# Batch normalisation, loads and stores on two rings: stores no longer wait for the store before them

## The chip, the cores and the metric

One core of a Trainium2 chip. The time is the device time of the slowest core of one execution, in microseconds (us), here that of the only core. Executions of one kernel on one chip lie within some 0.1 to 0.3% of each other; a run is compared with the runs of the kernel before on its own chip.

## The reference

`x` is float32 of 32 x 256 x 128 x 128 (537 MB); the result has the same shape.

```python
mean = running_mean.reshape(1, -1, 1, 1)
var = running_var.reshape(1, -1, 1, 1)
return gamma * (x - mean) / np.sqrt(var + eps) + beta      # gamma, beta reshaped likewise
```

For one channel this is `x * scale + shift`. The work is the traffic: each value is read once and written once.

## The kernel before

Comments on the lines are added for this text.

`x` is seen as 64 tiles of 128 partitions x 16,384 values (8.39 MB). Three buffers in the on-chip memory hold three tiles; VectorE (DVE) works in place. SP issues the loads (its ring is q1), ACT the stores (its ring is q10). Left out: the computation of scale and shift at the start, some 12 us beside the first load.

```python
NBUF = 3
...
for i in range(1, NT):                       # SP: loads
    s, turn = i % NBUF, i // NBUF
    if turn:
        nc.sync.wait_ge(stored[s], 16 * turn)            # L97: the buffer's last store has landed
    inst = nc.sync.dma_start(out=bufs[s][:], in_=xr[i]).then_inc(loaded[s], 16)     # L98
    if i >= 2:                                           # and the load before has landed
        inst._wait_ge(loaded[(i - 1) % NBUF], 16 * ((i - 1) // NBUF + 1))
...
def store(i, after):                         # ACT: stores
    s = i % NBUF
    inst = nc.scalar.dma_start(out=outr[i], in_=bufs[s][:]).then_inc(stored[s], 16) # L137
    inst._wait_ge(done, after)                           # the tile's compute is done

def turn_of_store(i):
    nc.scalar.wait_ge(stored[(i - 1) % NBUF], 16 * ((i - 1) // NBUF + 1))

compute(0, left)._wait_ge(early, 16)
compute(0, right)._wait_ge(loaded[0], 16)
store(0, 2)
for i in range(1, last):
    compute(i)._wait_ge(loaded[i % NBUF], 16 * (i // NBUF + 1))     # DVE
    turn_of_store(i)                                                # ACT: one store at a time
    store(i, i + 2)
...                                          # the last tile: 9216 columns on DVE, 7168 on ACT
store(last, last + 3)
```

## Time and profile before

| | kernel before |
|---|---|
| time, median of 3 runs | 2483.66 us (2483.18 to 2484.57) |
| span of the profiled run | 2484.7 us |
| busy: DVE, ACT | 23%, 0% |
| DMA engines busy, 30 to 2454 us | 1.00 |
| one load, issue to landing (median of 63) | 38.6 us |
| store issued after its tile's landing (median) | 16.9 us |

The last row holds the wait that the change takes out; the prediction shows the lines behind the table.

A second source is used throughout, the DMA packet records of the trace: start, length, size and ring of each packet, without the engine's number. Sums over all packets divided by 16 are "per engine". The order on one engine I rebuilt, by joining each packet to the engine whose last packet ended nearest its start; engines whose packets end at the same moment can be swapped in this, so sums are safer than any one row. In the rows below, L is a 65,536-byte packet of a load, S one of a store, l and s the small packet that ends an engine's part of a transfer; the number is the start in us, in the last two digits before the point. The kernel before, two of its 16 engines, around the landing at 1020.4 us and the store's issue at 1037.4:

```
L10.3 S12.7 L15.1 S17.6 l20.0 S20.0 S22.4 L24.8 S27.2 L29.6 S32.0 L34.5 s36.9 L36.9 L39.3 S41.7 L44.1 S46.5
L11.0 S13.4 l15.8 S15.8 S18.3 S20.7 S23.1 L25.5 S27.9 L30.3 s32.7 L32.8 L35.2 L37.6 L40.0 S42.4 L44.8 S47.2
```

Each ring has a gap between two transfers, and each gap is filled with packets of the other ring.

### The profile page before, as it was taken

To read this page: it belongs to the slowest core of one execution; us is meant where nothing else is said; L and a number is where in the kernel's file an instruction comes from. 1 tells how busy PE (TensorE), PEld (TensorE's weight loads), DVE (VectorE), ACT (ScalarE), POOL (GpSimd) and SP (SyncE) were. 2 spreads that over 40 slices of the span, in tenths; PEclk is the share of its full clock that TensorE was granted. 3 is DMA by queue.
4 is the path that set the end of the run, shared out by engine and by line. 5 is a ranking of instruction groups with operands and counts; after the bars stand their busy time and mean duration, and the time that the engine had idled before them with its cause. 6 is when DMAs were issued, how large, how long until landed. Compare 5 with 4: busy or idle time off the path is not lost.

```text
span 2484.7 us, 389 instructions
## 1 busy us (share of the span) xinstructions
DVE 564.0 (23%) x76; ACT 7.9 (0%) x3; POOL 0.2 (0%) x4
## 2 busy tenths in 40 slices
DVE  3121221212212222122221221212212122121221
ACT  0000000000000000000000000000000000000001
POOL 0000000000000000000000000000000000000000
DMA  9999999999999999999999999999999999999999
GB/s 422 423 439 434 430 436 435 437 428 437 435 436 432 433 438 429 436 434 431 434 427 437 437 426 439 436 432 430 436 438 430 433 427 438 430 430 437 436 426 406
DMA packets 18707, 1073.84 MB, mean 432 GB/s; under 512 B 2128, under 2 KB 2192, under 8 KB 2192
## 3 DMA queue, kind: packets, MB, share of 16 engines
q1 hardware_dynamic: 9488, 536.94, 50.1%
q10 hardware_dynamic: 9216, 536.88, 49.9%
q14 instruction: 3, 0.02, 0.0%
HBM read 536.94 MB, written 536.87 MB: 432 GB/s over the span
## 4 chain that ended last, share of the span: by engine, by line
DMA 99%; ACT 0%; SPq 0%; issue 0%; DVE 0%; DVEq 0%
DMA t<-in_x_dram 99%; ACT t L154 0%; SPq L87 0%; DVE rows L85 0%; SPq L91 0%; DVE eps_t L103 0%; DVEq L190 0%; SPq L66 0%
## 5 line engine op out<-in xcount | busy, mean ns | idle before, releaser
L126 DVE TENSOR_SCALAR t<-t,scale_t,shift_t 128x16384 f32<-128x16384 f32 (+2 forms) x65 | 560.5, 8624 | 1886.5 <-DMA t<-in_x_dram 1886.4
L154 ACT ACTIVATE t<-t,shift_t,scale_t 128x7168 f32<-128x7168 f32 x1 | 6.4, 6361 | 2442.7 <-DMA t<-in_x_dram 2442.7
L104 DVE STREAM_TRANSPOSE turned<-rows 32x1024 f32<-32x1024 f32 x1 | 1.2, 1233 | 7.1 <-DMA rows<-in_running_mean_dram 7.1
L111 ACT ACT_TABLE_LOAD x1 | 1.3, 1283 | 0.9 <-SPq L66 0.9
L85 DVE MEMSET rows<- 32x1024 f32 x1 | 0.9, 912 | 1.2 <-SPq L66 1.2
L109 DVE COPY par<-turned 32x8 f32<-32x8 f32 x4 | 0.6, 162 | 0.1
L111 ACT ACTIVATE std_t<-par,eps_t 128x2 f32<-128x2 f32 x1 | 0.3, 295 | 9.2 <-DVE par L109 9.2
L118 DVE RECIPROCAL rstd_t<-std_t 128x2 f32<-128x2 f32 x1 | 0.2, 166 | 0.4 <-ACT std_t L111 0.4
L121 DVE TENSOR_TENSOR shift_t<-par,ms_t 128x2 f32<-128x2 f32 x1 | 0.2, 163 | 0.0
L120 DVE TENSOR_TENSOR ms_t<-par,scale_t 128x2 f32<-128x2 f32 x1 | 0.2, 161 | 0.0
L119 DVE TENSOR_TENSOR scale_t<-par,rstd_t 128x2 f32<-128x2 f32 x1 | 0.2, 161 | 0.0
L179 POOL MEMSET const-bfloat16-1.0<- 128x1 bf16 x1 | 0.1, 102 | 0.0
L179 POOL MEMSET const-uint8-127<- 128x1 uint8 x1 | 0.1, 101 | 0.0
L179 POOL MEMSET const-float32-0.0<- 128x1 f32 x1 | 0.1, 99 | 0.2 <-issue 0.2
L179 POOL MEMSET const-float32-1.0<- 128x1 f32 x1 | 0.1, 98 | 0.0
L103 DVE MEMSET eps_t<- 128x1 f32 x1 | 0.1, 59 | 0.1
## 6 DMA issues: line engine op xcount, KB each, us to landing
t<-in_x_dram SPq DMA_DIRECT2D x1, 6144.0 KB, 19.4
t<-in_x_dram SPq DMA_DIRECT2D x1, 2048.0 KB, 7.6
out_dram<-t ACTq DMA_DIRECT2D x64, 38.6
t<-in_x_dram SPq DMA_DIRECT2D x63, 38.6
rows<-in_running_var_dram SPq DMA_DIRECT2D x1, 16.0 KB, 6.4
rows<-in_gamma_dram SPq DMA_DIRECT2D x1, 16.0 KB, 6.2
rows<-in_beta_dram SPq DMA_DIRECT2D x1, 16.0 KB, 5.9
rows<-in_running_mean_dram SPq DMA_DIRECT2D x1, 16.0 KB, 5.9
```

The lines of the kernel that those rows point to most:

```text
L85: zeroed = step(nc.vector.memset(rows[:], 0.0))
L103: step(nc.vector.memset(eps_t[:], eps))
L104: step(nc.vector.transpose(out=turned[:], in_=rows[:]), fetched, 16 * NPAR)
L109: placed = step(nc.vector.tensor_copy(out=flat[q * B : (q + 1) * B], in_=blocks[:, :, q, 0]))
L111: nc.scalar.activation(out=std_t[:], in_=var_t, func=mybir.ActivationFunctionType.Sqrt, bias=eps_t[:], scale=1.0,)._wait_ge(vec, placed).t ...
L118: step(nc.vector.reciprocal(out=rstd_t[:], in_=std_t[:]), act, 1)
L119: step(nc.vector.tensor_mul(out=scale_t[:], in0=gamma_t, in1=rstd_t[:]))
L120: step(nc.vector.tensor_mul(out=ms_t[:], in0=mean_t, in1=scale_t[:]))
L121: ready = step(nc.vector.tensor_sub(out=shift_t[:], in0=beta_t, in1=ms_t[:]))
L126: return nc.vector.tensor_scalar(out=t[:, cols], in0=t[:, cols], scalar1=scale_t[:, cb : cb + 1], scalar2=shift_t[:, cb : cb + 1], op0=myb ...
L154: nc.scalar.activation(out=t[:, VCOLS:], in_=t[:, VCOLS:], func=mybir.ActivationFunctionType.Identity, bias=shift_t[:, cb : cb + 1], scale ...
L179: nc = _bacc.Bacc("TRN2", target_bir_lowering=False, num_devices=1)
```

## The change

Its intent: a store is queued as soon as its tile is computed. ACT then never stands in front of a finished tile, and the stores' ring need not run empty between two stores. The loads keep their rule of one at a time.

```diff
-        def turn_of_store(i):
-            nc.scalar.wait_ge(stored[(i - 1) % NBUF], 16 * ((i - 1) // NBUF + 1))
-
         compute(0, left)._wait_ge(early, 16)
         compute(0, right)._wait_ge(loaded[0], 16)
         store(0, 2)
         for i in range(1, last):
             compute(i)._wait_ge(loaded[i % NBUF], 16 * (i // NBUF + 1))
-            turn_of_store(i)
             store(i, i + 2)
```

## The prediction

> **What bounds the kernel now.** I read the page's totals first, then its DMA part, then the waits of the two engines that issue transfers, then the order of time in one steady stretch and at the end. The page:
>
> ```profile
> DVE 564.0 (23%) x76; ACT 7.9 (0%) x3; POOL 0.2 (0%) x4
> ...
> DMA  9999999999999999999999999999999999999999
> ...
> q1 hardware_dynamic: 9488, 536.94, 50.1%
> q10 hardware_dynamic: 9216, 536.88, 49.9%
> q14 instruction: 3, 0.02, 0.0%
> HBM read 536.94 MB, written 536.87 MB: 432 GB/s over the span
> ```
>
> No compute engine is busy for more than 23% of the span. The 16 DMA engines are at 90% or more in all 40 slices, and the two rings (q1 the loads, issued by SP; q10 the stores, issued by ACT) share them 50.1% to 49.9%: together all of it. The stretches of time say how full this is (columns: stretch, its length, busy time of three engines, clock, DMA share, GB/s):
>
> ```profile
> 0.00:2.00 2.00, 0.79 (x1) 1.10 (x1) 0.20 (x4) 1.00 0.07 16
> 2.00:30.00 28.00, 11.79 (x13) 0.47 (x2) 0.00 (x0) 1.00 1.05 444
> 30.00:1020.00 990.00, 220.32 (x26) 0.00 (x0) 0.00 (x0) 1.00 1.00 433
> 1020.00:2010.00 990.00, 229.13 (x26) 0.00 (x0) 0.00 (x0) 1.00 1.00 433
> 2010.00:2454.40 444.40, 96.94 (x11) 0.00 (x0) 0.00 (x0) 1.00 1.00 433
> 2454.40:2461.40 7.00, 5.08 (x1) 6.36 (x1) 0.00 (x0) 1.00 0.91 393
> 2461.40:2481.40 20.00, 0.00 (x0) 0.00 (x0) 0.00 (x0) 1.00 0.97 419
> 2481.40:2484.70 3.30, 0.00 (x0) 0.00 (x0) 0.00 (x0) 1.00 0.00 0
> ```
>
> The DMA share is 1.00 from 30 us to 2454 us. What is idle lies at the two ends: 2 us before the first packet, 3.3 us after nearly the last. Every tile is 8.39 MB, moved in and out. In the DMA packet records each engine moves a tile as eight packets of 65,536 bytes; a packet takes 2.418 us, and successive packets of one engine start 2.414 us apart, for loads and stores alike. So a tile costs each engine 16 packets, 16 x 2.414 = 38.6 us, which is the step of the chain that ended last. 64 tiles x 38.6 = 2472 us is the floor that the traffic sets, and the span is 2485: at most 13 us (0.5%) can be had by any reordering of the same bytes.
>
> The waits, and one steady stretch:
>
> ```profile
> SPq L98 <- DMA t<-in_x_dram: 1378.8, 62, 48.0
> SPq L97 <- DMA out_dram<-t: 1009.0, 61, 16.8
> ```
> ```profile
> 1020.46 155.17 SPq L98 DMA_DIRECT2D t<-in_x_dram  x5
> 1020.47 8.81 DVE L126 TENSOR_SCALAR t<-t,scale_t,shift_t 128x16384 f32<-128x16384 f32 x1 [29.85 <-DMA t<-in_x_dram]
> 1037.40 155.24 ACTq L137 DMA_DIRECT2D out_dram<-t  x5
> ```
>
> A load is released at 1020.46 by the landing of the load before it (L98 has the later wait; the buffer's store, L97, had landed about 22 us earlier: 38.6 less 16.5). The compute ends at 1029.28, but its store goes only at 1037.40, when the store before it has landed: that wait of 8.1 us is what the change removes.
>
> **What the Trainium skill says.** The page "DMA: Bandwidth & Descriptors", section "Queues, rings and completion order", says that each DMA engine goes round robin between the rings it has work for, a whole packet at a time. The trace agrees: in the packet records an engine alternates load, store, load, store; where one ring is empty between two transfers (last landing, semaphore, next issue, first packet) it takes 3 to 5 packets in a row of the other ring, and in the steady stretch no engine shows an idle gap worth naming. Its section "Issuing engines are not separate DMA queues" says that transfers issued from several engines run on the same 16 DMA engines, and that this saves only issue time; the trace agrees (one store's issue is 0.34 us on ACT). Its section "Where 436 GB/s comes from" gives 435.2 GB/s as the ceiling of the ports into the on-chip memory; 16 engines at 65,536 bytes per 2.414 us are 434 GB/s, so the kernel already stands at it.
>
> **The change part by part.** It takes out 62 waits of ACT, nothing else: bytes, packets, compute and the loads' waits stay.
>
> 1. What the waits cost now. 62 x 8.1 us = 502 us of a store held back, all beside a busy DMA. A store that is held leaves its ring empty for a moment, and the engines then take load packets: nothing is lost on the path.
>
> 2. What comes in the steady state. A store is queued when its compute is done, behind the rest of the store before it in the same ring. The stores' ring has no gap at first while the loads' ring still has one (2 to 4 packets more for stores per turn), so stores gain on loads. That ends within a few tiles, when a store has nothing ahead of it on arrival: then it is compute, 8.8 us after the load's landing, that starts a store, and both rings have gaps of like size again. The period stays 16 packets, 38.6 us. Median landing time of stores goes from 38.6 to something between 38.6 and 46.7 (8.1 more at the front), back towards 38.6 once the gain is used up. The gap of the loads is still filled: at a load's end an engine has now 5 to 6 store packets left of the previous store; with stores 8.1 us earlier, about 3.4 of 16 slots, half of them stores, it has about 3 to 4 left, and the gap needs 3 to 5. It is near the edge, but the engines that need 5 are those ahead on loads, thus behind on stores.
>
> 3. What it does to the end. Before:
>
> ```profile
> 2415.80 8.81 DVE L126 TENSOR_SCALAR t<-t,scale_t,shift_t 128x16384 f32<-128x16384 f32 x1 [29.82 <-DMA t<-in_x_dram]
> 2432.75 0.34 ACTq L137 DMA_DIRECT2D out_dram<-t  x1
> 2454.43 6.36 ACT L154 ACTIVATE t<-t,shift_t,scale_t 128x7168 f32<-128x7168 f32 x1 [2442.73 <-DMA t<-in_x_dram]
> ...
> 2460.82 0.34 ACTq L137 DMA_DIRECT2D out_dram<-t  x1
> ```
>
> The last load lands at 2454.4, its compute ends at 2460.8; the last store but one lands at 2464.1, so it covers that compute and the DMA hardly idles. With the stores 8.1 us ahead, half rate gives 4.1 us of DMA work moved from after the last load to before it: the last load lands at 2458.5, its store is issued 6.39 us later, at 2464.9, while the store before still ends by 2464.1. From issue to first packet on an idle engine was 0.87 us (2460.82 to 2461.69), the eight packets take 19.4 us, the completion some 0.2, and 1.3 us pass from the last landing to the end of the span: 2464.9 + 0.87 + 19.4 + 0.2 + 1.3 = 2486.7, against 2484.7. Loss: about 2 us, uncovered compute at the end. If the gain of the stores stops at half of this (a store's first packet came 4.3 us after its issue when both rings had work), the loss is nearly 0.
>
> Sum: 0 in steady state, 0 to +2 us at the end; 2483.66 + 1.8 = 2485.5 us.
>
> **The rivals.**
> - Faster: the bubbles that the waits make between stores close, some per cent come back. For it: 62 x 8.1 us look like much. Against it: the DMA share is 1.00 with them. What could come back are the load steps of 38.7 to 39.4 us, some 7 us in all, which are small stalls; if longer queues hide half of them: 2480. Over 2% faster would be 2434, under the floor of 2472.
> - Slower, a new wait: the stores get so far ahead that at a load's landing the ring of stores is dry, and the DMA idles until the next load's first packet (2.6 to 4.3 us after its issue). Against it: a dry store ring lets loads run at full rate, which restores the lag. If it did happen for 1 us in each turn, +62 us: 2547.
> - Slower, loads crowded out: two stores in one ring take more than half. Against it: the rings take turns, not transfers. If so, a load that lands late delays its store too, and the rate of the sum would stay: 0 to +10 us.
>
> **Range and chances.** The traffic's floor puts a wall at -0.5%; below I take stall recovery of 4 us (2479.5). Above, 2 us at the end, with the engines less in step, 5 more: 2492. Faster by 2% is all but excluded (0.01), the dry ring is worth 0.03, the rest is the same.
>
> **What would show it.** Right: DMA share 1.00 between 30 and 2450 us, load steps still 38.6 (some early ones 40 to 43 while the stores gain), store issues 8.8 us after the load's landing in place of 16.9, SP's wait at L97 down from 16.5 towards 8 to 12 us a turn with L98's up by as much, the last load landing up to 4 us later, and a short idle stretch before the last store. Wrong: a DMA share under 0.99 in the middle, load steps over 39 us throughout, or stores landing in well over 46 us throughout.

## The result, and the profile after

| | before | after |
|---|---|---|
| time, median of 6 runs | 2484.03 us (2482.88 to 2485.29) | 2506.30 us (2503.28 to 2509.88) |
| span of the profiled run | 2484.7 us | 2504.6 us |
| store issued after its tile's landing | 16.9 us | 8.9 us |
| load packets over 2.418 us, summed, per engine | 5.2 us | 22.2 us |
| store packets over 2.418 us, summed, per engine | 0.1 us | 0.1 us |
| gaps in which an engine runs nothing, per engine | 0.2 us | 4.6 us (4.2 at the end) |

Below, the sum of the load packets' time over 2.418 us is called stretch, the time in which an engine runs nothing is called gaps, and the time from a tile's landing to the issue of its store is called lag. The ratio is 1.0090 (95% interval 1.0077 to 1.0103). Ratios are the mean time of one kernel's fast runs over that of the other's fast runs of the same rounds, so not quite the ratio of the medians quoted. The change costs 22 us, within 2% and clear of the noise. The prediction had 2485.5 us, with a range up to 2492.

The page of the changed kernel:

```profile
DMA  9999999999999999999999999999999999999998
...
q1 hardware_dynamic: 9488, 536.94, 50.4%
...
HBM read 536.94 MB, written 536.87 MB: 429 GB/s over the span
```

The same stretches of time as those of before (length, busy time of DVE, ACT, POOL, clock, DMA share, GB/s):

```profile
30.00:1020.00 990.00, 220.32 (x25) 0.00 (x0) 0.00 (x0) 1.00 1.00 429
1020.00:2010.00 990.00, 221.59 (x26) 0.00 (x0) 0.00 (x0) 1.00 1.00 431
2010.00:2475.00 465.00, 104.47 (x12) 0.00 (x0) 0.00 (x0) 1.00 1.00 430
2475.00:2482.00 7.00, 5.08 (x1) 5.78 (x1) 0.00 (x0) 1.00 0.46 197
2482.00:2502.00 20.00, 0.00 (x0) 0.58 (x1) 0.00 (x0) 1.00 0.97 419
```

The DMA share in the middle is 1.00 as before, yet the same full engines move 429 to 431 GB/s in place of 433. A share counts a packet as busy for as long as it lasts, so a packet that takes longer hides in it; the GB/s column shows it. At the end the share falls to 0.46 for 7 us, where it was 0.91.

The waits of SP for loads (L98) and for buffers (L97):

```profile
SPq L98 <- DMA t<-in_x_dram: 1832.0, 62, 48.2
SPq L97 <- DMA out_dram<-t: 575.1, 61, 16.5
```

Stores land earlier, as meant: L97 falls from 1009 to 575 us. L98 takes it all and more: 1379 to 1832 us. The chain that ended last (start, length), two steps of the kernel before and then four of the changed kernel:

```profile
1020.46 38.60 DMA t<-in_x_dram
...
1059.08 38.66 DMA t<-in_x_dram
```

```profile
994.84 37.20 DMA t<-in_x_dram
...
1032.06 41.02 DMA t<-in_x_dram
...
1073.09 36.61 DMA t<-in_x_dram
...
1109.72 41.03 DMA t<-in_x_dram
```

The even step of 38.6 us has become a long and a short one in turn, through the whole run: the 62 steps after the first two loads sum to 2423 us (53.1 to 2476.2), 39.1 us each, against 2402 us (52.9 to 2454.4) and 38.7. The stores follow the landings, 8.9 us after each:

```profile
1032.06 8.81 DVE L126 TENSOR_SCALAR t<-t,scale_t,shift_t 128x16384 f32<-128x16384 f32 x1 [28.40 <-DMA t<-in_x_dram]
1040.91 41.37 ACTq L137 DMA_DIRECT2D out_dram<-t  x2
```

One engine in the packet records over both kinds of step ("+" is a packet's length over 2.418 us, in ns):

```
S31.8 S34.3 L36.7 s39.1 L39.1 L41.5 L43.9 S46.3 L48.8 S51.2 L53.6 S56.0 L58.4 S60.8 L63.2 S65.7 l68.1
S68.1 S70.5 S72.9 s75.3 L75.3(+54) L77.8 L80.2 L82.6 L85.0(+560) S88.0 L90.4 S92.8
```

After the landing at 1073.1 this engine uses up the last store packets just as the next load comes (s75.3), and then has nothing but loads until 88.0. On all 16 engines together there is no store packet for 7.5 to 9 us in 29 of the long steps (kernel before: 6 to 7.5 us in each step). In those 29 the load packets are over length by 466 ns per engine at each; before, by 25. The packet before the first store packet bears most of it. Of the whole stretch of 22.2 us, 16.3 us lie in load packets that end within 14 us of a store's issue (before: 2.6 of 5.2).

The end of the changed kernel:

```profile
2407.28 37.04 ACTq L137 DMA_DIRECT2D out_dram<-t  x2
...
2476.22 6.36 ACT L150 ACTIVATE t<-t,shift_t,scale_t 128x7168 f32<-128x7168 f32 x1 [2464.56 <-DMA t<-in_x_dram]
...
2482.61 0.34 ACTq L137 DMA_DIRECT2D out_dram<-t  x1
```

The last load lands at 2476.2 in place of 2454.4, and the earlier stores end before the last store is issued: 4.2 us idle per engine.

The sum: 17.0 us more of stretched load packets and 4.4 us more of gaps are 21.4 us; the spans differ by 19.9. The rest goes the other way at the last store, which now starts on all engines together: its 16 parts land within 0.2 us, where they took 2.0.

### The profile page after: what moved, and what is told of

Its sections match the earlier page's. It is cut to its first block, busy times and chain, and to the rows that moved or that the text cites. A ratio compares the mean times of both kernels' runs of the same rounds, so it can differ in the third digit from the quotient of the medians.

```text
span 2504.6 us, 327 instructions
## 1 busy us (share of the span) xinstructions
DVE 564.1 (23%) x76; ACT 7.9 (0%) x3; POOL 0.2 (0%) x4
## 3 DMA queue, kind: packets, MB, share of 16 engines
q10 hardware_dynamic: 9216, 536.88, 49.5%
## 4 chain that ended last, share of the span: by engine, by line
DMA 99%; ACT 0%; SPq 0%; issue 0%; DVE 0%; DVEq 0%
DMA t<-in_x_dram 99%; ACT t L150 0%; SPq L87 0%; DVE rows L85 0%; SPq L91 0%; DVE eps_t L103 0%; DVEq L186 0%; SPq L66 0%
## 6 DMA issues: line engine op xcount, KB each, us to landing
out_dram<-t ACTq DMA_DIRECT2D x64, 39.8
```

## The experiments

Theory A: stores come too early. Theory B: two stores in one ring are served worse, whenever they come. All kernels gave the reference's result unless it is said otherwise. The runs e1, e3, e2 and e4 shared one chip (before: 2483.99 us); e5, e6, e7 and p1 another (2486.29); r1, r2, e9 and p2 a third (2486.72).

### e1_delay8: free stores, but late

```diff
+        # ACT, between the end of a tile's compute and its store: 8 x activation of a 128x1024 scratch tile
+            hold(i + 2)
+            nc.scalar.wait_ge(held, holds[0])
             store(i, i + 2)
```

> The changed kernel (stores never wait for a store), but ACT spends about 7 to 9 us on eight 128x1024 activations on a scratch tile between the end of a tile's compute and the issue of its store (128x7168 took 6.36 us, so 0.89 ns an element). So the store is issued about 17 us after the load's landing, as the removed wait did it. Theory A (the stores come too early: at a load's landing too few store packets are left, all engines run out of stores together and then take 4 to 5 loads in a row, of which some are stretched; plus 4.2 us idle at the end): back to 2482 to 2489 us, stretch of load packets back from 22 us to about 5 us per engine, no idle at the end. Theory B (two stores queued in one ring are served worse, whenever they come): stays at 2500 to 2510.

2488.56 us (ratio 1.0017, interval 1.0002 to 1.0032). Stores go 17.6 us after the landing; load packets are stretched by 7.2 us per engine, gaps are 0.2 us. The chain is even again:

```profile
1060.94 38.64 DMA t<-in_x_dram
...
1099.60 38.61 DMA t<-in_x_dram
```

Stores are as free as in the change, and ACT does useless work; still four fifths of the loss are gone. That is theory A's number. Theory B is not tested by it, though, since two stores hardly ever queue here. The times of stores from issue to landing in the changed kernel, in e1 and in e4 below:

```profile
DMA to landing us min/median/max: 20.7/39.8/44.3
```

```profile
DMA to landing us min/median/max: 22.9/38.0/40.6
```

```profile
DMA to landing us min/median/max: 22.6/49.5/51.5
```

In e1 stores follow each other at 38.7 us and land after 38.0, so that the store before has nearly always landed. In the changed kernel they follow at 36.7 and 41 us in turn and land after 39.8, so that every other store is queued some 3 us behind an unfinished one; in e3 it is the same.

### e3_delay4: half the delay

The same with four activations.

> As e1, with four activations, about 4 us. Theory A: between the two, 2484 to 2500, stretch of load packets between 5 and 22 us per engine. Theory B: 2500 to 2510.

2495.48 us (1.0054, 1.0037 to 1.0071). Stores 13.3 us after the landing, stretch 13.0 us. Between, as A has it (B's 2500 is missed). The steps still alternate:

```profile
1026.53 36.36 DMA t<-in_x_dram
...
1062.91 41.16 DMA t<-in_x_dram
```

### e2_wait_early: the wait kept, stores early

```diff
             if turn:
                 nc.sync.wait_ge(stored[s], 16 * turn)
+            if i == 2:
+                nc.sync.wait_ge(done, 3)      # once: tile 1 is computed
```

> The kernel before, wait of stores kept, but load 2 is held once until the compute of tile 1 is done (8.8 us later), so that the store before has landed by then and stores follow their compute at once. The hold itself costs 1 to 4 us of idle DMA, once. Theory A: the lag of stores stays small for the whole run, so 2498 to 2512, with steps of loads that alternate and load packets stretched by 15 to 25 us per engine, and 3 to 5 us idle at the end. Theory B: there is never a second store in the ring, so 2484 to 2490.

2490.33 us (1.0025, 1.0010 to 1.0040). A's number is missed clearly, B's by 0.3 us, which is less than the scatter of the runs. The stores settled at 12.1 us after the landing, not at 8.8 as I had meant: while the held load starts, it has the engines to itself and gains part of the lead back. Stretch is 7.2 us, gaps 3.6 us (1.7 from the hold, 1.6 at the end), and the steps stay even:

```profile
1029.49 38.73 DMA t<-in_x_dram
...
1068.24 38.70 DMA t<-in_x_dram
```

Set beside e3 on the same chip this says more than was asked: at a like lag (12.1 and 13.3 us) the stores that wait for each other run even steps with 7.2 us of stretch, the stores that wait for the landing alone alternate with 13.0. Of the 7.2 us, 3.2 fall in the first two turns after the hold; the rest of the run has 4.0, no more than the kernel before. So here a store at 12.1 us was not enough for the loss. Either the wait gave the stores' ring a time of its own, or it helped by keeping a second store out of the ring (theory B): e2 does not tell these apart.

### e5_wait_lag9: a second hold

```diff
+            if i in (2, 3):
+                nc.sync.wait_ge(done, i + 1)  # tile 2 is computed in two parts, load 3 waits for the first
```

> As e2 (the wait of stores kept), with a second hold once: load 3 waits for the first 5.08 us of tile 2's compute. Stores should then follow their load's landing by about 9 to 10 us (before: 16.9; e2: 12.1), near the compute's end (8.8). The holds cost 2 to 5 us of idle DMA once, and the end 3 to 4 us. Theory A1 (a small lag of the stores alone makes the loss): 2500 or more, stretch of load packets over 12 us per engine. Theory A2 (the loss needs stores that are started by the load's landing, so that turns of 41 and 36.6 us alternate; with the wait each ring keeps its own time): steps of 38.6 to 38.7, stretch 5 to 9 us per engine, 2488 to 2495.

2498.95 us (1.0051, 1.0036 to 1.0066): outside both. The lag settled at 12.1 us again, so the question was not put. Gaps are 8.6 us, of which 6.9 in the first tiles, stretch is 12.7 us, and the steps are even. It shows that with the wait kept this lag could not be brought lower by holds, and nothing on A1 against A2. Of the stretch, 3.6 us fall in the first turns after the holds; the rest, 9.2 us, is more than e2's 4.0 at the same lag, on another chip.

### e4_both_free: loads free as well

```diff
             inst = nc.sync.dma_start(out=bufs[s][:], in_=xr[i]).then_inc(loaded[s], 16)
-            if i >= 2:
-                inst._wait_ge(loaded[(i - 1) % NBUF], 16 * ((i - 1) // NBUF + 1))
```

> The changed kernel without the wait of a load for the load before it: both rings are queued freely, loads bound only by buffers. Theory A: loads come early, stores end late, the stores' ring seldom runs dry before the next store: 2478 to 2490. Theory B: two loads in one ring are served worse too: 2505 to 2530.

2505.35 us (1.0084, 1.0069 to 1.0099): A's number missed, B's met, but not for B's reason. Stretch is 5.6 us of loads and 5.4 us of stores; 12.9 us are idle at the end. In all turns a store is queued some 10 us before the one before it has landed (49.5 us from issue to landing, as shown above), and still the load packets are stretched no more than in the kernel before. This speaks against theory B as the cause of the change's stretch, which is all in load packets; it is no proof, since the loads are free here too.

```profile
2445.00:2465.00 20.00, 0.00 (x0) 0.00 (x0) 0.00 (x0) 1.00 0.98 423
2465.00:2480.00 15.00, 5.08 (x1) 6.36 (x1) 0.00 (x0) 1.00 0.14 61
```

Of the last load 14 engine parts landed from 2446.4 to 2450.5 us, two at 2473.0. With no load waiting for all parts of the one before, two engines had slipped 23 us behind, and at the end 14 engines waited for them. In the kernel before the parts of a load land within 4 to 5 us. In these runs the loads' rule of one at a time keeps the engines in step.

### e6_loads_free: the mirror of the change

The same edit on the kernel before (stores one at a time, loads free).

> The mirror of the change: the kernel before, stores one at a time, but a load waits for its buffer alone and not for the load before it. In e4 (both free) the stretch was low (about 10 us for both rings) and 13 us were idle at the end. If the free ring gains on the other, loads gain, stores end late and the end has no idle: 2478 to 2488. If loads are held to the landing of stores, as stores are to that of loads in the change: turns alternate, 2490 to 2510.

3240.03 us (1.3032, 1.3002 to 1.3062), far outside. What I had as the milder branch, loads held to the landing of stores, happened in full: compute, load and store start together, and then both rings are empty together.

```profile
1034.10 8.81 DVE L124 TENSOR_SCALAR t<-t,scale_t,shift_t 128x16384 f32<-128x16384 f32 x1 [42.09 <-DMA t<-in_x_dram]
1034.26 51.59 SPq L98 DMA_DIRECT2D t<-in_x_dram  x2
1034.32 51.61 ACTq L135 DMA_DIRECT2D out_dram<-t  x2
```

```profile
1000.00:2000.00 1000.00, 167.42 (x19) 0.00 (x0) 0.00 (x0) 1.00 0.88 328
```

Gaps are 363 us per engine, stretch is 310 us of loads and 84 us of stores. Here store packets are stretched too, and all through a transfer; why is not settled. Which of the two waits is kept matters: without this one the loss is 754 us, without the other 22.

### e7_end_split and r2_end_split: the end alone

```diff
-        store(last, last + 3)
+        # last tile in 4 pieces on DVE and ACT; its first 4096 columns are stored when they are done
+        ... dma_start(out=outr[last][:, :4096], in_=t[:, :4096]) ...
+        ... dma_start(out=outr[last][:, 4096:], in_=t[:, 4096:]) ...
```

> The changed kernel, but the last tile is computed in four pieces on two engines and stored in two, the first 2 MB about 2.8 us after the landing in place of the whole 6.4 us after it. This takes away only the idle 4.2 us at the end: 2502 to 2504 against the changed kernel's 2506, if that term is real and separate; 2506 if the end is idle for another reason. The stretch of load packets (22 us per engine) stays.

> e7 again, beside the changed kernel on the same chip (e7 ran beside the kernel before alone, on a chip where that took 2.3 us longer; its idle at the end was gone, but load packets were stretched 3.6 us more). If the idle end is a term of its own: 3 to 4 us less than r1. If it is only where the engines wait anyway: the same as r1 within 1.5 us.

> The changed kernel again, for a comparison on one chip with the three below: 2502 to 2510, idle at the end 4 us per engine, stretch of load packets 20 to 25 us per engine.

e7: 2510.38 us (1.0095) on a chip without the changed kernel beside it. So it was run again beside that: r1, the changed kernel, 2510.58 us (1.0094, 1.0080 to 1.0108); r2 2510.58 us (1.0097, 1.0082 to 1.0113). The idle end is gone in the profile, from 2.3 us per engine in r1 to 0.0 in r2. The stretch where the last tile is computed, first r1, then r2:

```profile
2475.00:2487.00 12.00, 5.08 (x1) 6.36 (x1) 0.00 (x0) 1.00 0.76 328
```

```profile
2475.00:2487.00 12.00, 5.27 (x2) 6.64 (x2) 0.00 (x0) 1.00 0.93 401
```

The profiled spans differ by that, 2508.4 and 2506.3, but the timed runs don't: both scatter over 6 us. A gain of 2 us is neither shown nor excluded. r1 missed its own numbers: the stretch is 27.9 us on this chip, the idle end 2.3 us and not 4. So these terms vary by chip or run.

### e9_delay12: a longer delay

e1 with eleven activations.

> As e1 with eleven activations, some 12 us, stores about 21 us after the load's landing. If the loss comes from stores that come too early, it stays gone: 2483 to 2490, stretch 4 to 8 us per engine, steps of 38.6 us. If e1 was good because its lag equals by chance that of the kernel before (16.9), it comes back: over 2492.

2493.28 us (1.0021, 1.0008 to 1.0033). By the number alone this is the second branch, 3 us over the first. But on this chip the kernel before took 2486.72 us and the changed kernel 2510.58, so that the loss is 6.6 us of 23.9, and the ratio is like that of e1. Stores go 20.9 us after the landing, stretch is 9.1 us, the steps are even after the first ten. I read it as the first branch on a slower chip: e1 was no lucky hit, and more delay brings nothing more. Most stores are queued here some 0.8 us behind an unfinished one (39.5 us from issue to landing, steps of 38.7), without the loss of the change; for theory B this is a weak test.

### p1_probe and p2_probe_read: what stretches a load packet

Their outputs are wrong, which doesn't matter for the times. Two loads are always queued, and every third tile alone is computed and stored, so that before each store the engines run nothing but loads for 40 us. In p2 the store is replaced by a load of the same size, on the same ring, into the same buffer.

```diff
-            inst = nc.scalar.dma_start(out=outr[i], in_=bufs[s][:]).then_inc(stored[s], 16)
+            inst = nc.scalar.dma_start(out=bufs[s][:], in_=xr[i]).then_inc(stored[s], 16)      # p2
```

> A probe with a wrong result on purpose: two loads are always queued, and only every third tile is computed and stored, so that the engines are load-only for some 30 us before each of 21 stores. Theory M1 (a store that arrives after all 16 engines have been load-only for 8 us or more stretches the load packet then running): over 300 ns per engine at each arrival, other load packets at 2.418 us. Theory M2 (the loads alone are slower than 2.418 us when no store runs, and the long turns show that): load packets stretched all through the load-only time. Theory M3 (the stretch belongs to loads that begin on a dry ring, one at a time): none at the arrivals here, under 60 ns per engine.

> The probe p1 with one change: in place of each store ACT issues a load of the same tile into the same buffer (wrong result on purpose), so that what arrives on the second ring after the long load-only time is a read and not a write. p1 showed about 700 to 1000 ns of stretch of the load packet before each arrival, per engine. If any arrival on an empty ring does that: the same here. If it takes the start of writing: under 100 ns.

In p1 the last load packet before the first packet of a store is over length by 689 ns in the mean where 18 load packets went before (214 cases; 1,003 and 685 ns for 17 and 19). The mean hides two kinds of start: summed from the last store packet before to 6 us after the first one of the next store, the stretch per engine is 23 to 100 ns at the first four of 20 starts and 287 to 1,858 ns at the other 16 (mean 1,274), all after 41 to 43 us of loads alone. In p2 the last one before the other ring's first packet is over by 4 ns (320 cases). The stretches from 200 to 1000 us, p1 first:

```profile
200.00:1000.00 800.00, 88.13 (x10) 0.00 (x0) 0.00 (x0) 1.00 1.00 428
```

```profile
200.00:1000.00 800.00, 96.94 (x11) 0.00 (x0) 0.00 (x0) 1.00 1.00 433
```

Again a DMA share of 1.00 in both, and 428 against 433 GB/s. An arrival on an empty ring does nothing by itself; here the stretch came only where the arrival was a write. But p2 differs in one more thing: its 16 engines stay in step (their first packets on the second ring start within 0.3 to 1.3 us of each other; in p1 within 0.9 to 2.4 us at the first four starts, within 2.1 to 4.1 at the others). Whether engines out of step are a part of the cause or a result of the stretch was not tested. Of p1's theories, M1 holds in the mean and not at each arrival; M2 falls, since p2 runs loads at full rate throughout; M3 falls, since p1 stretches with two loads queued.

### p3_probe_dose, p4_probe_dose, p5_probe_dose: how long must loads run alone?

Three attempts to vary the time of loads alone in steps, wrong results on purpose, two loads always queued and stores from an unchanging tile at set intervals:

```diff
+    # p3: 84 stores of 16 partitions;  p4: 84 of 128 x 2048;  p5: 35 whole tiles
+            inst = nc.scalar.dma_start(out=outr[...], in_=bufs[2][...]).then_inc(stored[2], 16)
```

> A probe with a wrong result on purpose: 64 loads of 8.39 MB, two always queued, and beside them 84 small stores of 1 MB (one packet for each engine) from a tile that never changes, issued by ACT after 4, 6, 8, 10, 12, 16 and 24 activations of 128x1024 (about 1.08 us each), twelve of each. Between two stores the engines so run loads alone for about 2 to 24 us. If the stretch at the start of writing grows with the time of loads alone, as 25 ns at 7 us (kernel before), some 500 at 8.6 us (changed kernel), 700 to 1000 at 40 us (p1) suggest: under 50 ns per engine for gaps of 4 and 6, hundreds from 8 to 10 on. If it depends on something else than that time (what loads and stores are where in their tiles): no order with the gap.

> p3 mended: there each small store took 16 partitions, and its packets ran some 6.7 us in place of 2.4, so that stores piled up and no gap was as meant. Here a small store takes 2,048 columns of all 128 partitions (1 MB, eight packets of 8,192 bytes for each engine). Same expectation: if the stretch at the start of writing grows with the time of loads alone, under 50 ns per engine for gaps of about 2 to 5 us and hundreds from some 8 us on; if something else decides, no order with the gap.

> p4 mended: there the rings took turns packet by packet, so that a store of 8,192-byte packets got one small packet for each 65,536-byte packet of a load and lasted 19 us; again no gap was as meant. Now 35 whole stores of 8.39 MB from a tile that never changes (eight packets of 65,536 bytes for each engine, some 38.7 us beside loads), issued after 38, 40, 42, 44, 48, 56 and 66 activations (about 41 to 71 us), five of each. So the loads run alone for about 2.5 to 33 us between two stores. If the stretch at the start of writing grows with that time: under 100 ns per engine at 2 to 7 us, hundreds from some 8 us on, 700 to 1000 at 30 us. If something else decides: no order with the gap.

None put the question. In p3 a store packet from 16 partitions ran 6.7 us in place of 2.4, and the stores piled up. In p4 the rings took turns packet by packet, one of 8,192 bytes for one of 65,536, so that a 1 MB store lasted 19 us and again they piled up. In p5, where loads were not held to all parts of the load before, engines slipped apart as in e4. In the 14 us from a store's issue the stretch is 10 to 1,790 ns per engine, and not in the order of the gap: 1,790 ns 1.5 us after the last store packet, 620 ns 31.5 us after it.

So the length of the time of loads alone remains a guess from the kernels before and after, and the kept traces speak against it as the only cause. In e3 loads ran alone for 9.2, 9.1 and 8.9 us in early turns with 1 ns of stretch or less (12.2 us in another: 283 ns), in e9 for 11.5, 11.0 and 9.5 us with at most 32 ns, in p1 four times for 42 us with at most 100. Something else must come to it; the runs don't show what.

### The account of all

Stretch and gaps per engine, from the packet records of each profiled run:

| | store after landing, us | stretch | gaps | sum | span | span less sum |
|---|---|---|---|---|---|---|
| before | 16.9 | 5.3 | 0.2 | 5.5 | 2484.7 | 2479.2 |
| after | 8.9 | 22.3 | 4.6 | 26.9 | 2504.6 | 2477.7 |
| r1 (after again) | 8.9 | 28.0 | 2.6 | 30.6 | 2508.4 | 2477.8 |
| e3, delay 4 | 13.3 | 13.1 | 0.2 | 13.3 | 2492.4 | 2479.1 |
| e1, delay 8 | 17.6 | 7.4 | 0.2 | 7.6 | 2487.0 | 2479.4 |
| e9, delay 12 | 20.9 | 9.2 | 0.2 | 9.4 | 2488.5 | 2479.1 |
| e2, wait kept | 12.1 | 7.4 | 3.6 | 11.0 | 2488.7 | 2477.7 |
| e5, wait kept | 12.1 | 13.0 | 8.6 | 21.6 | 2499.5 | 2477.9 |

The last column is the same within 2 us: these two terms account for the spans. This says where the time went, not why. No version beat the kernel before.

## Why the prediction was wrong, point by point

- **The bound** was right: the DMA engines, at their ceiling, with at most 13 us to gain. Nothing was gained.
- **Step 1** was right: the 62 waits of ACT cost nothing on the path. Taking them away gave no time back.
- **Step 2 failed.** It said: "The period stays 16 packets, 38.6 us." The period became 39.1 us in the mean, as 41 and 36.7 in turn. Its parts were partly right: stores go 8.9 us after the landing, L97's wait fell to 9.4 us a turn (575.1 / 61), the median landing time of stores is 39.8 us, and the count of store packets left at a landing, "near the edge" with 3 to 4, is what the records show (three, between this load's l68.1 and s75.3). Its count for the kernel before, 5 to 6, was one too high: the two rows show 4 and 5. Near this edge I looked for idle engines and dismissed them. The engines don't idle. They run out of stores all together, run loads alone for 7.5 to 9 us, and load packets are stretched as the next store starts. I had taken 2.418 us for a constant of a packet, "for loads and stores alike"; in the changed kernel it isn't. This term, 0 in my sum, measured 17.0 us.
- **The rival of the dry ring** had the right place and the wrong form and size. I put it at 0.03, because a dry ring "lets loads run at full rate, which restores the lag". It does: the next step is short (36.6), has store packets left, and the one after is long again. I had not seen that this makes two kinds of turn, nor that the next store's start then stretches the loads. My estimate of 1 us a turn (62 us) was for an idle DMA; the stretch is 17.0 / 62 = 0.3 us a turn.
- **Step 3** was right in kind: the end has uncovered compute, 4.2 us idle in place of some 2. The last load was to land 4.1 us later; it landed 21.8 us later, nearly all from step 2. The "+1.8" of the sum was picked within "0 to +2" and not worked out. The end is also less bad than its idle time, since the last store's parts now land together.
- **The signs that I named**: "load steps over 39 us throughout" came true in the mean; "a DMA share under 0.99 in the middle" did not, and could not, because the share counts stretched packets as busy.

What is shown: the change's loss lies in stretched load packets (17.0 us) and in the idle end (4.2 us), and issuing the free stores later takes most of it away (e1, e9; about half in e3). A read in the place of the write stretches nothing (p1, p2).

What stays open: why the same start of a store has 25 ns of stretch in the kernel before and 466 in the long turns of the change. A lag of 12.1 us alone did it in e2 not at all and in e5, on another chip, in part; the length of loads alone doesn't decide (e3, e9, p1). The alternation, the second store in the ring (theory B, against which e4 and, weakly, e9 speak) and engines out of step are candidates that no run takes apart. Open is also whether the idle end costs any measured time (r2).

## What to carry to other kernels

A wait that never holds up the bounding resource can still set when one stream runs against another; before it is taken out, ask what will time the stream then. Where loads and stores share saturated DMA engines, count the store packets that an engine has left when a load lands: here 4 or 5 went with the good time (the kernel before, e1) and 2 to 4 with the bad one, and a store 17 us after the landing was better than one 9 us after it, even when the delay was useless work. It is not needed that the engines never all run loads alone: in the kernel before they do so for 6 to 7.5 us in each turn. A DMA share of 1.00 does not say that the rate is held, so read the GB/s beside it.

## What the Trainium skill lacked or had wrong

- "DMA: Bandwidth & Descriptors" has nothing on reads that slow when writing starts beside them: the load packet before a store's first one was over its 2.418 us by 685 to 1,003 ns in the mean after 40 us of loads alone (p1), though hardly at the first four starts, and by 4 ns where a read came in place of the store (p2).
- The same page, section "Queues, rings and completion order", has the turns of the rings by whole packets, and these runs agree (in the rows above L and S take turns at 2.4 us). It gives 9 to 17 descriptors as a typical packet; here one record is one row of 65,536 bytes, 2.418 us. It doesn't say what follows for rings of unequal packets: one of 8,192 bytes came for each of 65,536, and a 1 MB store lasted 19 us beside loads (p4).
- The same page, section "Where 436 GB/s comes from", says that for transfers between HBM and the on-chip memory the HBM side, about 358 GB/s, binds. It works this out as half of what a stack gives to its two cores, but the sentence doesn't say that it needs both of them at work. One core alone moved 433 GB/s for 2,400 us here, reads and writes together; that fits the section's ceiling of 435.2 GB/s and its 425 GB/s for one 16 MB load, not this limit.
- Its "Rules for kernel authors" do not say that transfers which wait for all parts of the one before keep the engines in step: without it two engines slipped 23 us behind the others (e4), where parts of a load landed within 4 to 5 us before.
